# Strassen's algorithm in the down projection of an encoder layer's MLP, its products interleaved with the next group's up projection

## Chip, core and metric

The kernel runs on one core of a Trainium2 chip, with one launch. The metric is the device time of that launch in microseconds (us), the median of several runs. A difference of about 0.2% (5 us here) is what a measurement of this kernel can tell from no change. Five engines work side by side, each through its own list of instructions in order: TensorE (PE, matmul), VectorE (DVE), ScalarE (ACT), GpSimd (POOL) and SyncE (SP, which issues the transfers here).

## What is computed

One encoder layer on 512 tokens of width 2048, in float32: a token mixer (latent attention and a recurrent part), an output projection, and an MLP with 8192 hidden units. The change concerns the MLP.

```python
mix = jnp.concatenate([attn_out, rec_out], axis=-1) @ w_out[layer]
x = x + gate_a * _rmsnorm(mix, post_mix_g[layer])

h = _rmsnorm(x, pre_mlp_g[layer]) * (1.0 + scale_m) + shift_m
y = jnp.square(jax.nn.relu(h @ w_up[layer])) @ w_down[layer]
x = x + gate_m * _rmsnorm(y, post_mlp_g[layer])
```

`gate_m` is a part of `cond @ w_mod + b_mod`; the kernel keeps its product with `post_mlp_g` in a tile `G`, spread over all partitions.

## The kernel before

Float32 products are made from two reduced parts. Each operand is cast to a high part H by ACT (a CAST), and DVE subtracts H from the operand to give the low part L (`split` L205, `hl` L226). One product of a 128x128 stationary tile and a 128x512 moving tile is then three matmuls into the same accumulator (`mm3` L221: H·H, H·L, L·H). Weights come from memory in pieces of 512 KB into a ring of four tiles `raw`, and are split into rings of three `wH` and two `wL`, two DVE and two ACT instructions of 512 columns for each piece. `tc.high_priority` puts the loads and splits 35 places ahead in the scheduler's order.

**Ahead of the MLP**, `project_out` makes the output projection (tiles `wo`), and `residual(t)` takes token tile t (128 tokens) through the first residual sum (L973), the norm (ACT L976, DVE L978), 16 transposes on PE (`x2T`, L982, into a ring of three PSUM banks), the scaling to `hv` (DVE L991 and ACT L988) and the split of the result into `atH`/`atL` and `recH`/`recL`, which hold the MLP's input, feature-major.

**MLP** (L1005 to L1096). The hidden units are worked through in 16 groups of 512. `up(g)` makes 192 matmuls of 512 columns (16 k-tiles x 4 hidden tiles x 3) into four PSUM banks; `up(0)` is done in two token halves, 384 matmuls of 256 columns. ReLU by ACT, square by DVE and a split give `uH`, `uL`. `down(g)` makes 192 matmuls `dn` (4 column chunks x 4 token tiles x 4 k-tiles x 3), one PSUM bank for each token tile and chunk; DVE adds each bank into `y` (L1053, 16 of 512 columns a group; ACT copies in the first group, L1051). The order is up(g), then down(g-1). PSUM has a ring `mm` of five banks and a ring `sd` of three. The tile `G` is prepared in pieces (`units`, L1009), one after each up chunk of the groups from 2 on: sums over w_mod (`modacc`, L262), then a matmul with `ones` and two DVE operations with rows loaded from memory (L301 to L304).

**The end** is `down_last` for group 15: all eight pieces of w_down are loaded and split early, into `atH`/`recH`, which are free by then; then token tile by token tile 48 matmuls `dl`, the sum into `y` (L1080), the norm (L1082 to L1084) and the store (L1088).

Of the kernel before, what the change touches and what calls it, by code (L numbers as in the profile page):

```python
# [10 lines left out]
F32 = mybir.dt.float32  # L11
# [21 lines left out]
PRI = 35  # L33

# [12 lines left out]
def encoder_layer(ctx: ExitStack, tc: tile.TileContext, a, out):  # L47
# [13 lines left out]
    def psum(n_mm, n_sd):  # L61
        if banks:
            banks["ctx"].close()
        banks["ctx"] = ExitStack()
        banks["mm"] = banks["ctx"].enter_context(pool("mm", n_mm, space=PSUM))
        banks["sd"] = banks["ctx"].enter_context(pool("sd", n_sd, space=PSUM))
# [136 lines left out]
    def split(raw, n, parts=2):  # L203
        H = stream.tile([P, 1024], F32R, tag="wH", name="wH")
        L = stream.tile([P, 1024], F32R, tag="wL", name="wL", bufs=2)  # L205
# [34 lines left out]
    def mod_block(accs, spans, fin, own=None, pri=PRI):  # L240
# [11 lines left out]
        def step(c):  # L252
            def run():
                with tc.high_priority(offset=pri):
                    _, v = load(source(nk * c, nk), nk, w, own)
                    for k in range(nk):
                        kt = nk * c + k
                        if kt == 0:
                            st["acc"] = accs.tile([P, 1024], F32, tag="modacc", name="modacc", bufs=2)
# [33 lines left out]
    def to_row(dst, col, gv, gcol):  # L293
# [17 lines left out]
    with ExitStack() as ph:  # L311
# [251 lines left out]
        with pool("start", side="right") as stp:  # L563
# [8 lines left out]
            for i in range(len(bounds) - 1):  # L572
# [3 lines left out]
                mod.append(mod_block(hg, [(P * k0, w), (2048 + P * k0, w)],  # L576
# [77 lines left out]
        for i in range(4):  # L654
            units += mod_block(hg, [(3 * 2048 + 512 * i, 512), (4 * 2048 + 512 * i, 512)],
                               to_cols(blk(hb2, i), blk(hs2, i), blk(b_sm, i), blk(b_cm, i), blk(g_mlp, i), sdt))
# [282 lines left out]
    gp = ctx.enter_context(pool("gp"))  # L939
    G = gp.tile([P, D], F32, name="G")  # L940
    with ExitStack() as ph:
        wo = ph.enter_context(pool("wo"))
# [4 lines left out]
        for i in range(2):  # L947
            c = 2 * 2048 + 1024 * i
            units += mod_block(gp, [(c, 1024)], to_row(GA[:, 1024 * i:1024 * i + 1024], c, a["post_mix_g"], 1024 * i))
# [56 lines left out]
    with ExitStack() as ph:  # L1006
        ml = ph.enter_context(pool("ml"))
        y = ml.tile([P, NT, D], F32, name="y")
        units = []  # L1009
        for i in range(2):  # L1010
            c = 5 * 2048 + 1024 * i
            units += mod_block(gp, [(c, 1024)], to_row(G[:, 1024 * i:1024 * i + 1024], c, a["post_mlp_g"], 1024 * i))
        NG = FF // 512

        def up(g, halves=((0, 4),)):
            pss = [mmt(f"up{n}") for n in range(4)]
            for t0, t1 in halves:
                for k0 in range(0, KD, 2):
                    H, L = chunk([(wslice(w_up, k0, 2, 512 * g, 512), 512)], 2, 512)
                    interleave(units, 1 if g > 1 else 0)  # L1020
                    for n in range(4):
                        ns = slice(n * P, (n + 1) * P)
                        o = pss[n][:, t0 * P:t1 * P]
                        for k in range(2):
                            cH, cL, kk = cat(k0 + k)
                            mm3(o, H[:, k, ns], L[:, k, ns], cH[:, t0:t1, kk, :], cL[:, t0:t1, kk, :],
                                k0 + k == 0, k0 + k == KD - 1)
            uH = ml.tile([P, 4, S], F32R, tag="uH", name="uH", bufs=2)
            uL = ml.tile([P, 4, S], F32R, tag="uL", name="uL", bufs=2)
            for n in range(4):  # L1030
                r = ml.tile([P, S], F32, tag="relu", name="relu", bufs=2)
                nc.scalar.activation(r, pss[n], AF.Relu)
                nc.vector.tensor_tensor(r, r, r, ALU.mult)
                hl(uH[:, n, :], uL[:, n, :], r)
            return uH, uL

        def down(g, u):
            uH, uL = u
            for c in range(4):
                pss = [mmt(f"dn{t}") for t in range(NT)]  # L1040
                for k0 in range(0, 4, 2):
                    H, L = chunk([(wslice(w_down, 4 * g + k0, 2, 512 * c, 512), 512)], 2, 512)
                    for t in range(NT):
                        ts_ = slice(t * P, (t + 1) * P)
                        for k in range(2):
                            mm3(pss[t], uH[:, k0 + k, ts_], uL[:, k0 + k, ts_], H[:, k, :], L[:, k, :],
                                k0 + k == 0, k0 + k == 3)
                for t in range(NT):
                    yv = y[:, t, 512 * c:512 * c + 512]
                    if g == 0:  # L1050
                        nc.scalar.copy(yv, pss[t])  # L1051
                    else:
                        nc.vector.tensor_tensor(yv, yv, pss[t], ALU.add)  # L1053

        def down_last(g, u):
# [74 lines left out]
```

## Time and profile before

| quantity | before |
| --- | --- |
| median of 3 runs | 2499.7 us (2498.49 to 2500.56) |
| span of the profiled execution | 2501.2 us |
| PE busy | 2423.2 us (97%), 11702 matmuls and transposes |
| DVE busy | 1420.3 us (57%) |
| ACT busy | 835.8 us (33%) |
| moved by DMA | 341.81 MB, mean 137 GB/s |
| MLP | from 1073.88 us (first `up` matmul) to the end |

The profiled execution took 2501.2 us of span, 1.5 us above the median of the runs. Busy times of PE are sums of single instructions whose reported durations overlap (a 512-column matmul reports 0.39 us but the next begins 0.23 us later), so the page counts the union, and the pitch from start to start is what a matmul costs. Rows of the trace have the form: start, duration, engine, line, operation, out<-in, size, count, and in brackets the idle time just before with what ended it. A wait on an engine other than the one that sets the end costs nothing by itself.

### The profile page before, as it was taken

Reading aid. Unit: us, or ns where it says so; the run is one execution under the profiler, and the core shown is the slowest. Engines: PE = TensorE matmul, PEld = TensorE weight load, DVE = VectorE, ACT = ScalarE, POOL = GpSimd, SP = SyncE. Lnnn points to the kernel's source line nnn. Section 1 sums busy time; section 2 is a strip of 40 time slices with the busy share of each in tenths; the row PEclk is TensorE's granted clock in tenths of the full one; section 3 lists DMA queues with packets and bytes.
Section 4 is the critical chain, followed back from the end, with each engine's and each line's share of the span. In section 5 each row is a group of like instructions: output and inputs, shape, how many; then the busy total and the mean of one; then the engine's idle time right before and its main releaser. Section 6 shows DMA issues by size and latency. Waiting matters only on the chain.

```text
span 2501.2 us, 30421 instructions
## 1 busy us (share of the span) xinstructions
PE 2423.2 (97%) x11702; PEld 2011.8 (80%) x11702; DVE 1420.3 (57%) x2197; ACT 835.8 (33%) x1550; POOL 117.9 (5%) x127
## 2 busy tenths in 40 slices
PE   4999999999999999999999999999999999999998
PEld 3788898989877776788888888888888888888886
DVE  6974777677976765674454554434434433443456
ACT  5224333333454422563322222222222222222232
POOL 0110211111200000000000000000000000000000
PEclk9999999999999999999999999999999999999999
DMA  9863353445611177563544543333233333333334
GB/s 316 290 219 106 117 157 118 152 126 165 190 51 34 54 256 229 186 220 108 160 134 128 168 147 123 101 94 100 93 99 95 94 100 93 101 94 94 100 116 136
DMA packets 193228, 341.81 MB, mean 137 GB/s; under 512 B 16822, under 2 KB 65084, under 8 KB 191036
## 3 DMA queue, kind: packets, MB, share of 16 engines
q1 hardware_dynamic: 191888, 339.72, 43.3%
q8 instruction: 92, 1.51, 0.2%
q14 instruction: 52, 0.43, 0.1%
q10 hardware_dynamic: 1196, 0.16, 0.0%
HBM read 331.45 MB, written 8.39 MB: 136 GB/s over the span
## 4 chain that ended last, share of the span: by engine, by line
PE 65%; DMA 3%; DVE 2%; ACT 0%; issue 0%; DVEq 0%; ACTq 0%
PE up L224 9%; PE up L222 9%; PE up L223 9%; PE dn L222 9%; PE dn L224 9%; PE dn L223 9%; DMA raw<-in_w_mod_dram 2%; PE wo L223 1%; PE wo L224 1%; PE wo L222 1%; DVE modacc L262 1%; PE dl L222 1%; PE dl L224 1%; PE dl L223 1%; PE pT L888 1%; PE sc L870 1%
## 5 line engine op out<-in xcount | busy, mean ns | idle before, releaser
L209 DVE TENSOR_TENSOR wL<-raw,wH 128x512 fp32r<-128x512 f32 (+1 forms) x800 | 529.4, 700 | 664.6 <-issue 533.4
L208 ACT CAST wH<-raw 128x512 fp32r<-128x512 f32 (+1 forms) x800 | 457.7, 616 | 1258.9 <-PE up L223 463.2
L222 PE MATMUL dn<-wH,uH 128*128 128x512 f32 x960 | 374.2, 390 | 0.0
L223 PE MATMUL dn<-wL,uH 128*128 128x512 f32 x960 | 374.2, 390 | 0.0
L224 PE MATMUL dn<-wH,uL 128*128 128x512 f32 x960 | 373.6, 389 | 0.0
L262 DVE SCALAR_TENSOR_TENSOR modacc<-raw,cond,modacc 128x1024 f32<-128x1024 f32 x120 | 160.5, 1338 | 109.0 <-DMA raw<-in_w_mod_dram 108.4
L224 PEld LDWEIGHTS dn<-wH,uL 128*128 128x128 f32 x960 | 180.2, 188 | 38.3 <-issue 0.5
L223 PEld LDWEIGHTS dn<-wL,uH 128*128 128x128 f32 x960 | 180.2, 188 | 38.3 <-issue 0.7
L222 PEld LDWEIGHTS dn<-wH,uH 128*128 128x128 f32 x960 | 180.2, 188 | 37.7 <-issue 0.2
L224 PE MATMUL up<-recH,wL 128*128 128x512 f32 (+1 forms) x544 | 207.8, 382 | 0.0
L222 PE MATMUL up<-recH,wH 128*128 128x512 f32 (+1 forms) x544 | 207.6, 382 | 0.0
L223 PE MATMUL up<-recL,wH 128*128 128x512 f32 (+1 forms) x544 | 207.5, 381 | 0.0
L224 PE MATMUL up<-atH,wL 128*128 128x512 f32 (+1 forms) x544 | 203.9, 377 | 2.8 <-DVE wL L209 2.8
L222 PE MATMUL up<-atH,wH 128*128 128x512 f32 (+1 forms) x544 | 205.1, 378 | 0.0
L223 PE MATMUL up<-atL,wH 128*128 128x512 f32 (+1 forms) x544 | 204.7, 377 | 0.0
L1053 DVE TENSOR_TENSOR y<-y,dn 128x512 f32<-128x512 f32 x224 | 152.8, 685 | 80.2 <-PE dn L224 80.2
L224 PEld LDWEIGHTS up<-recH,wL 128*128 128x128 f32 x544 | 102.0, 188 | 22.1
L222 PEld LDWEIGHTS up<-recH,wH 128*128 128x128 f32 x544 | 102.0, 188 | 21.9
L223 PEld LDWEIGHTS up<-recL,wH 128*128 128x128 f32 x544 | 102.0, 188 | 21.9
L224 PEld LDWEIGHTS up<-atH,wL 128*128 128x128 f32 x544 | 102.0, 189 | 21.7 <-DVE wL L209 3.0
L222 PEld LDWEIGHTS up<-atH,wH 128*128 128x128 f32 x544 | 102.6, 189 | 18.9 <-issue 0.2
L223 PEld LDWEIGHTS up<-atL,wH 128*128 128x128 f32 x544 | 102.5, 188 | 18.9 <-issue 0.2
(352 smaller groups left out, 3943.9 us busy)
## 6 DMA issues: line engine op xcount, KB each, us to landing
raw<-in_w_up_dram SPq DMA_DIRECT2D x136, 512.0 KB, 3.7
raw<-in_w_mod_dram SPq DMA_DIRECT2D x128, 512.0 KB, 4.1
raw<-in_w_down_dram SPq DMA_DIRECT2D x128, 512.0 KB, 3.7
raw<-in_w_in_dram SPq DMA_DIRECT2D x128, 256.0 KB, 3.1
mraw<-in_w_mod_dram SPq DMA_DIRECT2D x48, 512.0 KB, 5.4
raw<-in_w_out_dram SPq DMA_DIRECT2D x40, 512.0 KB, 4.1
raw<-in_w_in_dram SPq DMA_DIRECT2D x24, 512.0 KB, 6.4
mraw<-in_w_mod_dram SPq DMA_DIRECT2D x32, 256.0 KB, 4.1
```

Source lines behind the costliest of these rows:

```text
L208: nc.scalar.copy(H[:, o], raw[:, o])
L209: nc.vector.tensor_tensor(L[:, o], raw[:, o], H[:, o].bitcast(F32), ALU.subtract)
L222: nc.tensor.matmul(o, s_h, m_h, start=first, stop=False)
L223: nc.tensor.matmul(o, s_h, m_l, start=False, stop=False)
L224: nc.tensor.matmul(o, s_l, m_h, start=False, stop=last)
L262: nc.vector.scalar_tensor_tensor(st["acc"][:, :w], v[:, k, :], cond[:, kt:kt + 1], st["acc"][:, :w], ALU.mult, ALU.add)
L870: nc.tensor.matmul(ps, QS[t][0:64, hd, :], KX[0:64, :], start=False, stop=True)
L888: nc.tensor.transpose(pt[:, k * P:(k + 1) * P], pe[:, k * P:(k + 1) * P], ident)
L1053: nc.vector.tensor_tensor(yv, yv, pss[t], ALU.add)
```

## The change

The down projection of groups 0 to 14 is made by Strassen's algorithm in Winograd's form. For each group and each of two column chunks the 4 k-tiles x 512 tokens of `u` are cut into blocks A (2 k-tiles x 256 tokens) and the w_down pieces into blocks B (256 x 512); seven products of blocks take the place of eight. Each product is 12 matmuls of 512 columns into a PSUM tile of two banks, `dn`; three of the seven go on in the accumulator of an earlier one. So a group's down projection has 14 products, 168 matmuls. Sums of blocks are made on DVE: four of A a group (128x512 each, in place in `u`) and eight of B (128x1024, in place in the loaded tiles). A second accumulator `V` takes the part that belongs to three quarters of the output and is added to `y` once, in `down_last`, by three operations of 128x2x1024.

Which instructions follow which is written by hand: three strings give for each group 22 steps, U for one piece of the next group's up projection (24 matmuls), D for one product. Weights are split two steps ahead (`LEAD`), loads of w_down run up to six products ahead into a ring `B` of five tiles. A piece is now split by one ACT and one DVE instruction of 1024 columns; H has a ring of four places and L one of three. PSUM is set up anew ahead of the MLP: four banks `up` and two sets `dn` of two banks. The pieces for `G` go through tiles of the ring `B` and through the sets `dn`. `up(0)` stays 384 matmuls of 256 columns, group 15 stays as it was (192 matmuls, now in the four `up` banks). The tiles of `to_row` move to a pool that is closed before the MLP, and a scratch area is made smaller, which moves addresses alone.

```diff
+FIRST = "UUUUDDUDDUDDUDDUDDDDDD"
+ROUND = "UDUDDUDUDDUDUDDUDUDDDD"
+LAST = "UUDUUDUDUDUDUDDDDDDDDD"
...
+    psum(8, 0)
...
+        V = ml.tile([P, 2, 1024], F32, name="V")
...
+        def btile(name):
+            return ml.tile([P, 1024], F32, tag="B", name=name, bufs=NB)
+
+        def ubank(n):
+            return banks["mm"].tile([P, 512], F32, tag="up", name=f"up{n}", bufs=4)
+
+        def dset(name):
+            return banks["mm"].tile([P, 1024], F32, tag="dn", name=name, bufs=2)
...
+                    bg = btile("modbg")
+                    nc.sync.dma_start(bg[:, 0:512],
+                                      a["b_mod"][0:1, col + o:col + o + 512].partition_broadcast(P)[:, 0, :])
...
+                    ps = dset("modr")
+                    nc.tensor.matmul(ps[:, 0:512], ones, acc[:, o:o + 512], start=True, stop=True)
...
+            split_form("A11", A11)
+            split_form("A22", A22)
+            nc.vector.tensor_tensor(A22, A21, A22, ALU.add)
+            split_form("S1", A22)
+            split_form("A12", A12)
+            nc.vector.tensor_tensor(A21, A11, A21, ALU.subtract)
+            nc.vector.tensor_tensor(A11, A22, A11, ALU.subtract)
+            nc.vector.tensor_tensor(A12, A12, A11, ALU.subtract)
+            split_form("S4", A12)
+            split_form("S3", A21)
+            split_form("S2", A11)
...
+            goes_on = {2: 0, 3: 1, 6: 4}.get(f)
+            X = sets[f] = sets.pop(goes_on) if goes_on is not None else dset(f"dn{f}")
+            for t in range(2):
+                o = X[:, 512 * t:512 * t + 512]
+                ts_ = slice(t * P, (t + 1) * P)
+                for k in range(2):
...
+                    nc.tensor.matmul(o, sh, mh, start=first, stop=False, skip_group_check=skip)
+                    nc.tensor.matmul(o, sh, ml_, start=False, stop=False, skip_group_check=skip)
+                    nc.tensor.matmul(o, sl, mh, start=False, stop=last, skip_group_check=skip)
...
+            if g == 0 and fresh:
+                nc.scalar.copy(dst, Xv)
+            else:
+                nc.vector.tensor_tensor(dst, dst, Xv, ALU.add)
...
+            nc.vector.tensor_tensor(y[:, 0:2, 1024:], y[:, 0:2, 1024:], V, ALU.add)
+            nc.vector.tensor_tensor(y[:, 2:4, :1024], y[:, 2:4, :1024], V, ALU.add)
+            nc.vector.tensor_tensor(y[:, 2:4, 1024:], y[:, 2:4, 1024:], V, ALU.add)
...
+            fm = make_forms(hidden(pss))
+            pss = [ubank(i) for i in range(4)]
+            for _ in range(22):
+                ahead(n + 1 + LEAD)
+                what, _, i = steps[n]
+                H, L = wts.pop(n)
+                if what == "U":
+                    up_mms(pss, i, H, L, 0, NT)
+                    if g > 0:
+                        interleave(units, 1)
+                else:
+                    product(i, fm, H, L)
+                n += 1
+        down_last(NG - 1, pss)
```

Up to the end of the output projection the instructions stand in the same order on every engine. Three places show what moves behind it.

On PE at the start of the MLP (`wo` output projection, `up` the first up projection, `x2T` transposes of token tiles 2 and 3), before, in the middle of the first half of up(0), whose first matmul directly follows the last `wo`:

```order
L222 MATMUL up_8957<-atH,wH 128x256
L223 MATMUL up_8957<-atL,wH 128x256
L224 MATMUL up_8957<-atH,wL 128x256
L982 MATMUL x2T<-ident,xr 128x128 x12
L222 MATMUL up_8954<-atH,wH 128x256
L223 MATMUL up_8954<-atL,wH 128x256
L224 MATMUL up_8954<-atH,wL 128x256
```

and now:

```order
L230 MATMUL wo_8659<-wH,atH 128x512
L231 MATMUL wo_8659<-wL,atH 128x512
L232 MATMUL wo_8659<-wH,atL 128x512
L992 MATMUL x2T<-ident,xr 128x128 x32
L230 MATMUL up_8961<-atH,wH 128x256
L231 MATMUL up_8961<-atL,wH 128x256
```

The 32 transposes, which stood in five lots among the matmuls of up(0), now all stand ahead of its first one.

On DVE in the middle of the MLP, where down(g-1) runs, before (`dn` banks added to `y`, `wL` splits of weights, `modacc` a sum for G):

```order
L1053 TENSOR_TENSOR y<-y,dn_11573 128x512
L209 TENSOR_TENSOR wL<-raw,wH 128x512 x2
L1053 TENSOR_TENSOR y<-y,dn_11574 128x512
L209 TENSOR_TENSOR wL<-raw,wH 128x512 x2
L1053 TENSOR_TENSOR y<-y,dn_11643 128x512
L1053 TENSOR_TENSOR y<-y,dn_11644 128x512
L1053 TENSOR_TENSOR y<-y,dn_11645 128x512
L209 TENSOR_TENSOR wL<-raw,wH 128x512 x2
L1053 TENSOR_TENSOR y<-y,dn_11646 128x512
```

and now, around the four products that close a group (L1093 squares, `fL` splits of blocks of A, `dn_13843` the fourth product's set, `dn_13962` the fifth and seventh product's, `dn_13982` the sixth's):

```order
L1191 TENSOR_TENSOR y<-y,dn_13823 128x2x512
L1093 TENSOR_TENSOR u<-u 128x1024
L236 TENSOR_TENSOR fL<-u,fH 128x512
L236 TENSOR_TENSOR wL<-B_13552,wH 128x1024
L1093 TENSOR_TENSOR u<-u 128x1024
L236 TENSOR_TENSOR wL<-B_13651,wH 128x1024
L1191 TENSOR_TENSOR y<-y,dn_13843 128x2x512
L236 TENSOR_TENSOR fL<-u,fH 128x512
L1191 TENSOR_TENSOR y<-y,dn_13962 128x2x512
L236 TENSOR_TENSOR wL<-raw,wH 128x1024
L236 TENSOR_TENSOR wL<-B_13837,wH 128x1024
L1191 TENSOR_TENSOR V<-V,dn_13982 128x2x512
```

The additions of PSUM into `y` are now of two banks and stand among squares and splits of the next group, where before they stood between splits alone.

On DVE at the end, before (`atL`, `recL` the held splits of w_down, `dl` the last group's banks):

```order
L228 TENSOR_TENSOR atL<-raw,atH 128x1024
L228 TENSOR_TENSOR recL<-raw,recH 128x1024 x3
L1053 TENSOR_TENSOR y<-y,dn_18100 128x512
L228 TENSOR_TENSOR recL<-raw,recH 128x1024
L1053 TENSOR_TENSOR y<-y,dn_18101 128x512
L1053 TENSOR_TENSOR y<-y,dn_18102 128x512
L1053 TENSOR_TENSOR y<-y,dn_18103 128x512
L1080 TENSOR_TENSOR y<-y,dl_18207 128x512
```

and now (`upl` the last group's banks, L1210 to L1212 the additions of `V`):

```order
L236 TENSOR_TENSOR fL<-u,fH 128x512 x2
L236 TENSOR_TENSOR atL<-lraw,atH 128x1024
L1191 TENSOR_TENSOR y<-y,dn_17825 128x2x512
L236 TENSOR_TENSOR atL<-lraw,atH 128x1024 x3
L236 TENSOR_TENSOR recL<-lraw,recH 128x1024 x3
L1210 TENSOR_TENSOR y<-y,V 128x2x1024
L236 TENSOR_TENSOR recL<-lraw,recH 128x1024
L1211 TENSOR_TENSOR y<-y,V 128x2x1024
L1212 TENSOR_TENSOR y<-y,V 128x2x1024
L1226 TENSOR_TENSOR y<-y,upl_17929 128x512
```

Seven of the eight held splits now stand behind the last product's addition, and the three additions of `V` ahead of the first addition of `upl`.

## Rows read from the trace of the kernel before

**Rows 1.** The page: busy time, share, instructions; granted TensorE clock in 40 slices.

```profile
PE 2423.2 (97%) x11702; PEld 2011.8 (80%) x11702; DVE 1420.3 (57%) x2197; ACT 835.8 (33%) x1550; POOL 117.9 (5%) x127
PEclk9999999999999999999999999999999999999999
```

**Rows 2.** Busy per stretch: PE, PEld, DVE, ACT, POOL, clock, DMA share, GB/s.

```profile
1136.60:2446.80 1310.20, 1310.20 (x5730) 1074.69 (x5729) 581.67 (x863) 354.45 (x616) 0.00 (x0) 1.00 0.36 111
2000.00:2087.00 87.00, 87.00 (x382) 71.45 (x381) 36.03 (x56) 22.79 (x40) 0.00 (x0) 1.00 0.32 97
```

**Rows 3.** Waits from 1130 to 2400: total us, times, longest us.

```profile
ACT wH L208 <- PE up L223: 447.6, 104, 5.0
```

**Rows 4.** Timeline of PE (start, duration, what): down matmuls, then the last twelve.

```profile
1999.81 0.39 PE L222 MATMUL dn<-wH,uH 128*128 128x512 f32 x1
...
2006.38 0.39 PE L224 MATMUL dn<-wH,uL 128*128 128x512 f32 x1
...
2488.73 0.39 PE L222 MATMUL dl<-recH,uH 128*128 128x512 f32 x1
...
2491.29 0.40 PE L224 MATMUL dl<-recH,uL 128*128 128x512 f32 x1
```

**Rows 5.** Timeline of PE at the start of the MLP.

```profile
1073.88 0.28 PE L222 MATMUL up<-atH,wH 128*128 128x256 f32 x1
...
1083.57 0.38 PE L224 MATMUL up<-atH,wL 128*128 128x256 f32 x1 [2.82 <-DVE wL L209]
...
1121.77 0.28 PE L224 MATMUL up<-recH,wL 128*128 128x256 f32 x1
...
1127.89 0.40 PE L222 MATMUL up<-atH,wH 128*128 128x512 f32 x1
```

**Rows 6.** Timeline of DVE: scaling and split of tokens 0, 1; residuals of 2, 3.

```profile
1057.61 0.73 DVE L991 TENSOR_SCALAR hv<-x2T,hs,hb 128x128 f32<-128x128 f32 x2
...
1060.83 1.29 DVE L228 TENSOR_TENSOR recL<-hv,recH 128x512 fp32r<-128x512 f32 x2
1062.04 0.73 DVE L991 TENSOR_SCALAR hv<-x2T,hs,hb 128x128 f32<-128x128 f32 x2
...
1078.05 4.86 DVE L973 SCALAR_TENSOR_TENSOR mix<-mix,r,xr 128x1024 f32<-128x1024 f32 x4
...
1086.03 1.28 DVE L978 TENSOR_SCALAR xr<-mix,r 128x2048 f32<-128x2048 f32 x1
```

**Rows 7.** Timeline of PE after a wait, the first and the last slow matmul.

```profile
1067.45 0.65 PE L982 MATMUL x2T<-ident,xr 128*128 128x128 f32 x4 [2.48 <-ACT hv L988]
1067.86 0.67 PE L223 MATMUL wo<-wL,atH 128*128 128x512 f32 x1
...
1071.31 0.44 PE L223 MATMUL wo<-wL,atH 128*128 128x512 f32 x1
```

**Rows 8.** Two stretches with or behind a wait of PE, columns as in rows 2.

```profile
1050.00:1055.00 5.00, 3.99 (x24) 3.46 (x25) 5.00 (x12) 4.42 (x8) 0.00 (x0) 1.00 0.90 304
...
1085.00:1090.00 5.00, 5.00 (x32) 5.00 (x31) 4.68 (x10) 3.04 (x7) 0.00 (x0) 0.66 0.68 216
```

**Rows 9.** Groups by line and shape, 1136 to 2380: busy us, mean ns, idle before.

```profile
L1053 DVE TENSOR_TENSOR y<-y,dn 128x512 f32<-128x512 f32 x208 | 142.1, 685 | 77.0 <-PE dn L224 77.0
...
L1032 ACT ACTIVATE relu<-up 128x512 f32<-128x512 f32 x56 | 33.4, 596 | 11.4 <-PE up L224 11.4
...
L303 DVE TENSOR_TENSOR G<-modr,modb 128x512 f32<-128x512 f32 x4 | 2.8, 690 | 3.5 <-DMA modb<-in_b_mod_dram 3.1 <-PE modr L301 0.4
```

**Rows 10.** The same from 2380 to the end, DVE, 1024 columns.

```profile
L228 DVE TENSOR_TENSOR recL<-raw,recH 128x1024 fp32r<-128x1024 f32 x4 | 4.9, 1226 | 2.3 <-ACT recH L227 2.2
```

**Rows 11.** The same, ACT.

```profile
L227 ACT CAST recH<-raw 128x1024 fp32r<-128x1024 f32 x4 | 4.2, 1049 | 4.3 <-DMA raw<-in_w_down_dram 4.3
```

**Rows 12.** Timeline of DVE at 2443: a split of 1024 and its follower.

```profile
2443.57 1.23 DVE L228 TENSOR_TENSOR recL<-raw,recH 128x1024 fp32r<-128x1024 f32 x1 [1.03 <-ACT recH L227]
2444.71 0.68 DVE L1053 TENSOR_TENSOR y<-y,dn 128x512 f32<-128x512 f32 x1
```

More of the change, by code (lines that the diff above doesn't have):

```diff
@@ L291, in to_cols, with to_row @@
         return fin
[L293 removed]
+    def to_row(gp, dst, col, gv, gcol):
         def fin(acc):
@@ L1037, in down @@
[L1037 to L1053, printed above, removed]
@@ new lines, in encoder_layer, with form_tiles, hidden @@
+        FORMS = ["A11", "S1", "A12", "S4", "S3", "S2", "A22"]
+        def form_tiles(f):
+            return [ml.tile([P, 2, HALF], F32R, tag=f"f{x}{f}", name=f"f{x}", bufs=1) for x in "HL"]
+        def hidden(pss):
+            u = ml.tile([P, 4, S], F32, tag="u", name="u", bufs=1)
+            for n in range(4):
+                nc.scalar.activation(u[:, n, :], pss[n], AF.Relu)
+            for n in (0, 2):
+                nc.vector.tensor_tensor(u[:, n:n + 2, :], u[:, n:n + 2, :], u[:, n:n + 2, :], ALU.mult)
+            return u
@@ new lines, in encoder_layer, with down_loads, product @@
+        loaded = [0]
+        def down_loads(q):
+            while loaded[0] < min(q, NP):
+                s, f = divmod(loaded[0], 7)
+                for b in LOADS.get(f, []):
+                    down_load(s, b)
+                loaded[0] += 1
+        sets = {}
+        def product(q, fm, H, L):
+            s, f = divmod(q, 7)
+            g, c = divmod(s, 2)
+            fH, fL = fm[FORMS[f]]
+            goes_on = {2: 0, 3: 1, 6: 4}.get(f)
[3 more added lines that the diff above has]
+                ts_ = slice(t * P, (t + 1) * P)
+                for k in range(2):
+                    first, last = k == 0 and goes_on is None, k == 1
+                    sh, sl, mh, ml_ = fH[:, k, ts_], fL[:, k, ts_], H[:, k, :], L[:, k, :]
+                    skip = goes_on is not None
+                    nc.tensor.matmul(o, sh, mh, start=first, stop=False, skip_group_check=skip)
+                    nc.tensor.matmul(o, sh, ml_, start=False, stop=False, skip_group_check=skip)
+                    nc.tensor.matmul(o, sl, mh, start=False, stop=last, skip_group_check=skip)
+            cs = slice(512 * c, 512 * c + 512)
+            c2 = slice(1024 + 512 * c, 1024 + 512 * c + 512)
+            dst, fresh = [(V[:, :, cs], True), (y[:, 2:4, c2], True), (y[:, 0:2, cs], True), (y[:, 0:2, c2], True),
+                          (y[:, 2:4, c2], False), (V[:, :, cs], False), (y[:, 2:4, cs], True)][f]
+            Xv = X.rearrange("p (t n) -> p t n", t=2)
+            if g == 0 and fresh:
+                nc.scalar.copy(dst, Xv)
+            else:
+                nc.vector.tensor_tensor(dst, dst, Xv, ALU.add)
@@ L1057, in down_last @@
+        def down_last(g, pss):
+            u = hidden(pss)
+            uu = []
+            for n in range(4):
+                fH, fL = [t.rearrange("p k s -> p (k s)") for t in form_tiles(FORMS[n])]
+                hl(fH, fL, u[:, n, :])
+                uu.append((fH, fL))
             held = []
```

177 lines of the change are left out of this document (125 added, 52 removed).

## Prediction

> **What bounds the kernel now.** I read the page first, then the stretch of the MLP, then the waits, then single rows. The page shows PE busy for 97% of the span at full clock in nearly every slice, DVE for 57% and ACT for 33% [rows 1]. In the MLP it is stricter: from 1136.6 to 2446.8 PE is busy in all of the 1310.2 us, at a granted clock of 1.00, the upper level of 2.4 GHz, while DVE is busy 581.7 us and ACT 354.5 us [rows 2]. The waits say the same from the other side: ACT, the engine that casts the weights, waited 447.6 us for PE to free a buffer, and no wait of PE of any size is listed [rows 3]. So between 1136 and 2447 time is the number of matmuls times their pitch, and the other engines have slack. One matmul of the down projection costs (2006.38 - 1999.81) / 29 = 0.2266 us, not its reported 0.39; with `recH` as stationary tile it is (2491.29 - 2488.73) / 11 = 0.2327 [rows 4]. Outside that stretch, at the start of the MLP and at its end, PE depends on chains through DVE and ACT, and the change moves work there too.
>
> **What is removed.** 15 groups x (192 - 168) = 360 `dn` matmuls of 512 columns, all on the path that sets the end: 360 x 0.2266 = **-81.6 us**. The up projection, the last group and what lies ahead of the MLP keep their counts. The new stationary tiles are splits of blocks of `u` as before; I take the same pitch. Were it 0.2327, the 15 x 168 = 2520 remaining products would cost 2520 x 0.0061 = 15.4 us more.
>
> **Start of the MLP: +16 us.** Before, `up(0)` started at 1073.88, at once behind the output projection, and ended at 1127.89, with one wait of 2.82 us inside [rows 5]; it worked on tokens 0 and 1 while tokens 2 and 3 went through the residual on DVE and ACT. Now PE has the 32 transposes of tokens 2 and 3 ahead of the first up matmul, and these need the norms. The chain in the old trace: the four residual sums run 1078.05 to 1082.91, and the scaling of token 3 begins at 1086.03 [rows 6]. Without the weight splits that stood between, I put its end at 1086.7. Then come eight units of scaling and split, in pairs, through a ring of three PSUM banks, so the last transposes wait for the third pair's scaling. A pair took 1062.04 - 1057.61 = 4.43 us [rows 6] with weight splits between; these are gone from the list. Of DVE's own work a pair holds two lots of 0.73 and one of 1.29, 2.7 us, and between the ends of 2.7 and 4.4 I take 3.95, near the upper one, as each step there waits for ACT and back. So the third pair begins at 1086.8 + 7.9 = 1094.7, its scaling ends at 1096.6, and the first up matmul stands at about 1097. 384 matmuls of 256 columns cost (1127.89 - 1121.77) / 52 = 0.1177 each [rows 5], since 52 matmuls lie between, so 45.2 us. A wait of some 20 us is followed by a spell at the lower clock: behind a wait of 2.48 us eight steps took 1071.31 - 1067.86 = 3.45 us instead of 1.81 [rows 7], so 1.7 us more. End: 1097 + 45.2 + 1.7 = 1143.9 against 1127.89, **+16**. Ends: 12, with pairs at 2.7 us, and 22, with a pair at 4.43 and one or two waits such as the 2.82 us for the splits, which now stand on DVE behind the whole chain.
>
> **The groups: +1 us.** By 1024 columns a DVE operation reports 1.226 us [rows 10] but its follower starts 2444.71 - 2443.57 = 1.14 us after it [rows 12]; two of 512 take 1.29 in a row, so 0.6 each [rows 6]. DVE's list in a group: 22 splits, 8 sums of B, 14 additions, 2 squares, 46 x 1.14 = 52.4, and 11 operations of 512, 6.7; 59 us. PE: 96 up matmuls at 0.2266, 96 at 0.2327 and 168 products, 82.2 us. ACT has fewer instructions than before for the same columns (1.05 us for 1024 [rows 11]). DVE fits with 23 us to spare, so it is order that can hurt. The addition of two banks is not in the trace: one bank costs 0.685 [rows 9], so two lie between 1.14 (SBUF, 1024 columns) and 1.37 (twice); I take 1.14, the row of the same size. A product lasts 12 x 0.2266 = 2.72 us, and one that opens a set waits until the set before it in the ring of two is added. I walked one group through; only one place is tight, its four closing products. Counted from the start of the last up piece: its banks close at 1.4, 2.8, 4.2 and 5.5; the second ReLU (0.596 [rows 9]) ends at 3.7; then DVE has in order square (4.9), form split (6.2, behind ACT's cast), weight split (7.35), square (8.5), weight split (9.6), and the fourth product's addition to 10.8. The sixth product wants that set at 5.54 + 2 x 2.74 = 11.0. So 0.2 us of margin: no wait at my prices. At the full 1.226 for each of the five operations of 1024 each group waits 0.25 us, with 1.37 for the addition besides 0.5: 4 to 8 us in all. Taken: 1, ends 0 and 8. Cover: the weight splits are two steps ahead of PE; transfers are the same 16 pieces of 512 KB a group.
>
> **The pieces for G: +3 us.** The sums come over the same ring B as w_down and the row through a set `dn`; the next product but one waits until DVE has added the bias rows, which come by DMA into a tile that must first be free. Before, DVE idled 3.1 us for these rows [rows 9], hidden as PE had other banks. Now that idle time reaches PE: 3, ends 0 and 8 (two blocks, each once the 3.1 and a product's length, with overlap).
>
> **The end: +10 us.** From the last up piece PE has nine products, 24.5 us, and 48 matmuls of token tile 0, 11.0; then, at 35.5, the fifth tile wants a bank that the first addition of `upl` must free. DVE has in that time 2 squares, 7 splits, 4 sums, 9 additions and 8 held splits, 30 x 1.14 = 34.2, four splits of 512, 2.4, and three additions of V at twice 1.14, 6.8: 43.4. With 0.3 to start and 0.6 for the addition that frees the bank: 44.3, so PE stands for 8.8 us; a slow spell behind it adds 1.7 [rows 7]. Taken 10; ends 6 (the first square and two splits run before the piece ends) and 14 (1.226 for each). Before, the held splits had run early and PE did not wait. The norm and the stores behind the last matmul are the same.
>
> **Sum.** -81.6 + 16 + 1 + 3 + 10 = -51.6. On the profiled span 2501.2 that is 2449.6; the runs' median is 1.5 below that span, so I give 2499.7 - 51.6 = **2448 us**. With the ends of the four terms (18 to 52 against 30) the forecast's own range is 2436 to 2470.
>
> **Rivals.**
> 1. *Cheap ends.* The chain of tokens 2 and 3 overlaps better than in any row, and DVE works off more of the last list before the last up piece ends: terms 10, 0, 0 and 4, so 2432. For it: DVE's own work in a pair is 2.7 us only. Against: the pairs alternate between DVE and ACT.
> 2. *A slow spell in every group.* If the tight place does make PE wait and the clock falls to its lower level (1.2 GHz) each time, 1.7 us x 14 and the waits of 0.25, 3.5: +26, so about 2473. Against it: in 1050 to 1055 PE idled 1.0 us and the clock stayed at 1.00; it fell to 0.66 in 1085 to 1090 behind 2.82 us [rows 5, 8]. My walk gives no wait over 0.5.
> The Trainium skill, "TensorE: Matmul & The Clock Gate", section "A second HAM failure mode: psum-queue depth-cycling", speaks against this change: cycling through PSUM banks leaves PE idle for short moments between groups of matmuls, often enough that the clock swings. The rows at 1050 do not bear it out for one wait of that size; nothing here shows repeated ones.
> 3. *The gain does not arrive whole, by pitch.* Products at 0.2327: 2448 + 15 = 2463. Against: the rise is seen with `recH` alone.
> 4. *Slower than before: PE waits for its two sets.* In each group six products open a set close behind another. If the two-bank addition or its queue is late at three of them by enough to bring a slow spell, that is 3 x 1.7 x 15 = 77 us and more: about 2525. It decides from two such spells a group (2 x 1.7 x 15 = 51, the whole net gain), or from an addition of 3.0 us, at which DVE's 59 + 14 x 1.9 passes PE's 82 by 3.4 a group. For it: only two sets. Against: the rows put the addition at 1.14 to 1.37, at which the tightest place waits 0.5 us at most and the others not at all.
>
> **Chances.** Forecast with its own range 0.64; rival 1 below it 0.10; rival 2 0.12; rival 3 0.05, inside or just by the range; rival 4 0.06; within 0.2% (2494.7 to 2504.7, about what a measurement can tell from no change) 0.03, a mixture of 2 and 4. So faster 0.91, same 0.03, slower 0.06. The range 2434 to 2475 takes in rivals 2 and 3 and leaves about 0.2 out.
>
> **What will show it.** In the profile after: `dn` matmuls 2520, pitch 0.2266; the first `up` at about 1097 and the first 512-column `up` at 1144; PE busy without gaps in a group of 82.2 us, clock 1.00; DVE's two-bank addition at 1.2 to 1.4 us; a PE wait of about 9 us for DVE at the fifth `upl` tile. The prediction is wrong if PE shows a wait in every group, if the clock in the groups falls under 1.00, or if the first `up` starts soon after 1074.

## The result

| | before | changed |
| --- | --- | --- |
| median of 4 runs | 2499.1 us (2495.2 to 2500.6) | 2454.9 us (2451.4 to 2456.2) |
| ratio | | 0.982, 95% interval 0.9806 to 0.9835 |
| span of the profiled execution | 2501.2 us | 2449.6 us |
| PE busy | 2423.2 us (97%) | 2348.0 us (96%) |
| DVE busy | 1420.3 us (57%) | 1783.2 us (73%) |

The kernel is 44 us (1.8%) faster by the medians. The forecast was 2448 us, range 2434 to 2475, from a span of 2449.6; the span came out at 2449.6. That the two agree to a tenth is chance, as the ledger below shows: several terms missed by 1 to 4 us and cancelled. The profiled execution of the changed kernel is also the fastest of its four runs (the other three lie 3 to 5 us above it), while that of the kernel before, with a span of 2501.2, is longer than any of the four runs beside it. So the two traces lie 51.6 us apart and the medians 44.2; the 7 us between are scatter of single executions, and the ledger can't tell in which of its rows they lie.

The page of the changed kernel, beside [rows 1]:

```profile
PE 2348.0 (96%) x11342; PEld 1944.7 (79%) x11342; DVE 1783.2 (73%) x2203; ACT 932.9 (38%) x1423; POOL 119.2 (5%) x127
...
PEclk9999999999999999989999999999999999999998
```

PE has 360 instructions fewer, DVE as many as before but 363 us more to do, since more of them have 1024 columns. The clock has a lower slice at the start of the MLP and one at its end.

All waits of PE behind the output projection (total us, times, longest us):

```profile
PE x2T L992 <- DVE xr L988: 10.4, 1, 10.4
PE x2T L992 <- ACT hv L998: 6.3, 3, 2.9
PE upl L230 <- DVE y L1226: 3.6, 1, 3.6
PE upl L231 <- DVE recL L236: 2.2, 2, 1.7
PE dn L1180 <- DVE G L1047: 1.8, 3, 0.9
PE upl L231 <- DVE atL L236: 1.1, 2, 0.7
PE dn L1180 <- ACT wH L235: 0.7, 1, 0.7
PE dn L1181 <- DVE wL L236: 0.5, 1, 0.5
```

Three places are named, and they are the three of the forecast: the transposes ahead of the first up projection, the pieces for G, and the last group. No other wait is listed in the groups.

Where the 51.6 us between the two spans lie, by the starts of the same matmuls in both traces (the ledger's rows stand here and in the next sections; those of before are [rows 4, 5] and the first `dn` behind the last up piece of before, at 2403.69):

| stretch on PE | before | after | matmuls saved | beyond that |
| --- | --- | --- | --- | --- |
| up to the end of the output projection | 1073.9 | 1070.2 | | -3.7 |
| up(0) | 54.0 | 71.0 | | +17.0 |
| first 512-column up to the end of the last up piece | 1275.8 | 1218.4 | 276, -62.5 | +5.1 |
| from there to the end of the last matmul | 87.8 | 80.5 | 84, -19.0 | +11.7 |
| norm and stores behind it | 9.7 | 9.5 | | -0.2 |

```profile
2403.69 0.40 PE L222 MATMUL dn<-wH,uH 128*128 128x512 f32 x1
```

```profile
1069.97 0.39 PE L232 MATMUL wo<-wH,atL 128*128 128x512 f32 x1
...
1080.74 2.79 PE L992 MATMUL x2T<-ident,xr 128*128 128x128 f32 x12 [10.38 <-DVE xr L988]
...
1093.64 0.56 PE L230 MATMUL up<-atH,wH 128*128 128x256 f32 x1
...
1141.21 0.40 PE L230 MATMUL up<-atH,wH 128*128 128x512 f32 x1
...
2359.35 0.40 PE L232 MATMUL up<-recH,wL 128*128 128x512 f32 x1
...
2405.14 0.79 PE L230 MATMUL upl<-atH,fH 128*128 128x512 f32 x1 [3.56 <-DVE y L1226]
...
2439.82 0.40 PE L232 MATMUL upl<-recH,fL 128*128 128x512 f32 x1
```

The first `dn` behind the last up piece of before, and then the timeline of PE after the change: the output projection's last matmul, the wait, the first up matmul at 1093.64, the first of 512 columns at 1141.21, the last up matmul, the wait for the first addition of the last group, and the last matmul.

The groups by stretch (PE, PEld, DVE, ACT, POOL busy; clock, DMA share, GB/s), then the end:

```profile
2359.59:2440.05 80.46, 72.40 (x301) 56.69 (x299) 70.20 (x84) 28.01 (x52) 0.00 (x0) 0.96 0.43 137
1141.21:2359.59 1218.38, 1216.60 (x5303) 994.06 (x5302) 912.10 (x864) 440.29 (x498) 0.00 (x0) 1.00 0.37 116
```

In the groups PE is busy all but 1.8 of 1218.4 us at a clock of 1.00, as in [rows 2]; DVE, then at 44%, is now at 75%. At the end DVE is busy 70.2 of 80.5 us and PE stands for 8.

### The profile page after: what moved, and what is told of

It reads as the page before. It is cut to its first block, busy times and chain, and to the rows that moved or that the text cites. A ratio compares the mean times of both kernels' runs of the same rounds, so it can differ in the third digit from the quotient of the medians.

```text
span 2449.6 us, 29645 instructions
## 1 busy us (share of the span) xinstructions
PE 2348.0 (96%) x11342; PEld 1944.7 (79%) x11342; DVE 1783.2 (73%) x2203; ACT 932.9 (38%) x1423; POOL 119.2 (5%) x127
## 4 chain that ended last, share of the span: by engine, by line
PE 62%; DMA 3%; DVE 3%; ACT 1%; issue 1%; DVEq 0%; ACTq 0%
PE up L232 10%; PE up L230 10%; PE up L231 10%; PE dn L1180 8%; PE dn L1182 8%; PE dn L1181 7%; DMA raw<-in_w_mod_dram 2%; PE wo L231 1%; PE wo L232 1%; PE wo L230 1%; DVE modacc L273 1%; PE pT L899 1%; PE sc L881 1%; PE upl L230 0%; PE upl L231 0%
## 5 line engine op out<-in xcount | busy, mean ns | idle before, releaser
L235 ACT CAST wH<-B 128x1024 fp32r<-128x1024 f32 x210 | 221.1, 1054 | 499.3 <-PE up L231 194.3
L236 DVE TENSOR_TENSOR wL<-B,wH 128x1024 fp32r<-128x1024 f32 x210 | 256.5, 1222 | 185.4 <-issue 69.8
L1180 PE MATMUL dn<-wH,fH 128*128 128x512 f32 x840 | 329.3, 392 | 2.5 <-DVE G L1047 1.8
L1182 PE MATMUL dn<-wH,fL 128*128 128x512 f32 x840 | 327.5, 390 | 0.0
L1181 PE MATMUL dn<-wL,fH 128*128 128x512 f32 x840 | 326.8, 389 | 0.5 <-DVE wL L236 0.5
L216 ACT CAST wH<-raw 128x512 fp32r<-128x512 f32 (+1 forms) x288 | 163.2, 611 | 340.9 <-PE wo L232 59.5
L217 DVE TENSOR_TENSOR wL<-raw,wH 128x512 fp32r<-128x512 f32 (+1 forms) x288 | 199.1, 725 | 88.0 <-issue 44.6
L236 DVE TENSOR_TENSOR wL<-raw,wH 128x1024 fp32r<-128x1024 f32 x136 | 165.9, 1221 | 95.0 <-issue 43.0
L1181 PEld LDWEIGHTS dn<-wL,fH 128*128 128x128 f32 x840 | 157.7, 188 | 34.7 <-DVE wL L236 1.0
L1191 DVE TENSOR_TENSOR y<-y,dn 128x1024 f32<-128x1024 f32 x142 | 172.2, 1212 | 0.1
```

The lines of the kernel that those rows point to most:

```text
L216: nc.scalar.copy(H[:, o], raw[:, o])
L217: nc.vector.tensor_tensor(L[:, o], raw[:, o], H[:, o].bitcast(F32), ALU.subtract)
L235: nc.scalar.copy(h_out, src)
L236: nc.vector.tensor_tensor(l_out, src, h_out.bitcast(F32), ALU.subtract)
L1180: nc.tensor.matmul(o, sh, mh, start=first, stop=False, skip_group_check=skip)
L1181: nc.tensor.matmul(o, sh, ml_, start=False, stop=False, skip_group_check=skip)
```

## The experiments

### The start of the MLP: what holds back the first up projection

The forecast put the +16 us down to the new order on PE, in which all transposes stand ahead of the first up matmul. This run takes that away: the first up projection uses banks of the old PSUM rings.

```diff
-    psum(8, 0)
...
-        pss = [ubank(n) for n in range(4)]
+        pss = [mmt(f"up{n}") for n in range(4)]
...
+        u = hidden(pss)
+        psum(8, 0)
```

> The first up projection writes into banks of the old PSUM rings, and PSUM is set up anew only behind its ReLU; nothing else is altered. Theory (the new set-up of PSUM ahead of the first up projection is what puts the 32 transposes of tokens 2 and 3 ahead of it, and that order costs the time): the first up matmul follows the last matmul of the output projection at once, up(0) takes 54 us instead of 71.0, and the kernel is 15 to 18 us faster than the changed one: span 2432 to 2435, ratio to the kernel before about 0.975. Rival (the residual chain of tokens 2 and 3 sets the time whatever the order, and the second half of up(0) waits for it): up(0) stays over 65 us, less than 6 us are gained.

Measured: 2451.3 us, ratio 0.9816 (0.9801 to 0.983), against 0.982 for the change itself: nothing gained that the runs can tell. These are the numbers that the rival named, but not its cause, as the run with both locks off shows below. The order did change, and the time went elsewhere:

```profile
1068.90 0.28 PE L230 MATMUL up<-atH,wH 128*128 128x256 f32 x1
...
1082.98 2.82 PE L992 MATMUL x2T<-ident,xr 128*128 128x128 f32 x12 [7.21 <-DVE xr L988]
...
1100.56 0.58 PE L232 MATMUL up<-atH,wL 128*128 128x256 f32 x1 [6.27 <-DVE wL L236]
...
1141.13 0.50 PE L230 MATMUL up<-atH,wH 128*128 128x512 f32 x1
```

The first up matmul now follows the output projection at once, at 1068.90, but the third piece stands at 1100.56 for a low part from DVE, and up(0) ends at 1141.13, 72.2 us after it began. DVE's list of that stretch shows why:

```profile
1097.60 0.69 DVE L236 TENSOR_TENSOR recL<-hv,recH 128x512 fp32r<-128x512 f32 x1
1098.68 0.69 DVE L236 TENSOR_TENSOR recL<-hv,recH 128x512 fp32r<-128x512 f32 x1 [0.39 <-ACT recH L235]
1099.29 3.49 DVE L236 TENSOR_TENSOR wL<-raw,wH 128x1024 fp32r<-128x1024 f32 x3
```

The third and all later splits of w_up stand behind the last split of tokens 2 and 3. In the code, the change gives the splits an extra H and an extra L tile (`xH`, `xL`) in the MLP's own pool; the third L is the first to go there. By the code that pool is opened when the residual's is closed, so its tiles can lie where the residual's were and then wait for them; no row shows the addresses, and it is the next two runs that show the effect. So there is a second lock. One run takes off only this one, another both (and has the additions of V moved, next section).

```diff
+            if not own:
+                H = stream.tile([P, 1024], F32R, tag="wH", name="wH", bufs=3)
+                L = stream.tile([P, 1024], F32R, tag="wL", name="wL", bufs=NWL)
+                hl(H, L, src)
+                return [t.rearrange("p (k n) -> p k n", k=2) for t in (H, L)]
...
-            return split_next(raw)
+            return split_next(raw, g > 0)
```

> The splits of the first up projection use only the rings that exist before the MLP (three H, two L), not the extra H and L tile that lie in the memory which the residuals of tokens 2 and 3 still hold; PSUM is set up anew where the change has it. Theory (two locks, each enough by itself to hold the first up projection back: the order of the transposes through PSUM, and these tiles; the run with the PSUM edit alone gained under 2 us): this edit alone gains under 3 us as well, the first up matmul stays behind the transposes at 1090 or later. Rival (the tiles are the only true cause, the transposes' order follows them): up(0) ends some 15 us earlier than in the changed kernel.

Measured, one run: 2456.3 us, and the first up matmul at 1091.31 behind all transposes, up(0) 71.1 us long. The rival, that the tiles alone are the cause, falls.

> PSUM set up behind the first up projection, its splits in the old rings alone, and the additions of V moved as in the run on them. Theory (two locks): up(0) starts with the end of the output projection and takes 52 to 58 us instead of 71 to 72.8, as before the change; against the run with the additions of V moved 13 to 18 us less: span 2426 to 2431, ratio to the kernel before 0.971 to 0.974. Rival (with both locks off DVE, which now splits by 1024 columns among the residual's steps, sets the time): 62 us and more, span over 2436.

Measured: 2436.1 us, ratio 0.9758 (0.9742 to 0.9775), 8.8 us under the run with V alone, which is less than expected; but the first up projection did what the theory says:

```profile
1069.86 0.28 PE L230 MATMUL up<-atH,wH 128*128 128x256 f32 x1
...
1123.91 0.50 PE L230 MATMUL up<-atH,wH 128*128 128x512 f32 x1 [2.16 <-ACT u L1095]
...
1574.55 0.79 PE L1184 MATMUL dn<-wH,fH 128*128 128x512 f32 x1 [6.16 <-DVE G L1046]
1575.14 0.63 PE L1185 MATMUL dn<-wL,fH 128*128 128x512 f32 x1
```

up(0) takes 1123.91 - 1069.86 = 54.05 us, as before the change [rows 5]: 17 us back. The residual chain of tokens 2 and 3 is the same as in the change, so it is not what sets the time by itself. Of the 17 us, 7.4 were lost again in the groups (1225.4 us against 1218.0 in the run with V alone): the wait of 6.16 and a spell at the lower clock (pitch 0.43 from 1575.14 on). The run with only the ring edit shows that longer wait for G as well (6.32 us). So each lock by itself holds the start back by the full 17 us, and only both together free it.

### The end: the list of DVE behind the last up piece

```diff
-            nc.vector.tensor_tensor(y[:, 0:2, 1024:], y[:, 0:2, 1024:], V, ALU.add)
-            nc.vector.tensor_tensor(y[:, 2:4, :1024], y[:, 2:4, :1024], V, ALU.add)
-            nc.vector.tensor_tensor(y[:, 2:4, 1024:], y[:, 2:4, 1024:], V, ALU.add)
...
+                    if (t, c) in ((0, 2), (1, 3), (2, 1)):
+                        v = {0: y[:, 0:2, 1024:], 1: y[:, 2:4, :1024], 2: y[:, 2:4, 1024:]}[t]
+                        nc.vector.tensor_tensor(v, v, V, ALU.add)
```

> The three additions of V stand behind the first additions of the last group's banks of the token tile that needs them, instead of ahead of all. Theory (DVE's list between the last up piece and the fifth bank is what PE waits for): 6.6 us leave that list, the wait of 3.56 us at the fifth bank and the slow spell behind it go, the shorter waits for the held splits stay: 4 to 6 us faster than the changed kernel, span 2444 to 2446. Rival (the held splits, with the loads behind them, are what comes last): the wait stays where it is by over half, under 2 us gained. Second rival: the additions only move the wait to the later token tiles: the fifth bank is free, but waits of 2 us stand at token tiles 1 to 3, nothing gained.

Measured: 2444.9 us, ratio 0.9789 (0.9775 to 0.9804), 6.4 us under the run with the PSUM edit of the same chip and 10 under the changed kernel's own median. The waits of its last group:

```profile
PE upl L231 <- DVE atL L236: 1.1, 2, 0.7
PE upl L231 <- DVE recL L236: 0.9, 2, 0.8
PE upl L230 <- ACT recH L235: 0.8, 1, 0.8
PE dn L1181 <- DVE wL L236: 0.5, 1, 0.5
PE dn L1180 <- ACT wH L235: 0.4, 1, 0.4
```

The wait of 3.56 us at the fifth bank is gone; 3.7 us for splits stay. Nothing turned up at the later token tiles. The spell at a pitch of 0.43 did not go with the wait, as the theory had it. It stands at the same place, behind two short waits, in the profiled execution of this run:

```profile
2396.88 0.50 PE L230 MATMUL upl<-recH,fH 128*128 128x512 f32 x1 [0.81 <-ACT recH L235]
2398.14 0.50 PE L231 MATMUL upl<-recL,fH 128*128 128x512 f32 x1 [0.76 <-DVE recL L236]
...
2399.57 0.63 PE L230 MATMUL upl<-atH,fH 128*128 128x512 f32 x1
```

The spell lasts until 2402.56. So of the 5.8 us between the spans (2449.6 and 2443.8) 4.4 lie behind the last up piece, which is what the waits shrank by. With both this and the PSUM edit alone:

> Both edits together. Theory: they touch different ends of the MLP, so the gains add: 20 to 24 us faster than the changed kernel, span 2426 to 2430, ratio to the kernel before about 0.972. Rival: part of one is given back in the other (for instance in transfers): under 17 us.

Measured: 2446.8 us, ratio 0.9796 (0.9779 to 0.9812), no better than V alone. That was to be expected once the PSUM edit by itself gave nothing; it is the same miss a second time. Here the last group has no such spell.

### The pieces for G

```diff
+        def begin():
+            st["acc"] = accs("modacc")
+            nc.sync.dma_start(st["acc"], bias)
+            nc.vector.tensor_scalar(st["acc"], st["acc"], 1.0 / P, None, ALU.mult)
...
-                    nc.vector.tensor_tensor(d, ps[:, 0:512], bg[:, 0:512], ALU.add)
-                    nc.vector.tensor_tensor(d, d, bg[:, 512:1024], ALU.mult)
+                    nc.vector.tensor_tensor(d, ps[:, 0:512], d, ALU.mult)
...
+        nc.sync.dma_start(G, a["post_mlp_g"][0:1, :].partition_broadcast(P)[:, 0, :])
```

> On top of the run with both locks off: the row b_mod for G is loaded into the tile of the sums before they begin (scaled by 1/128, so that the sum over partitions gives it once), and the gain row straight into G; so no load stands between the matmul with ones and the product that wants its set. Theory (PE's waits of 0.31, 0.48 and 6.16 us behind the additions for G, and the slow spell behind the longest, come from these loads): these waits go, 6 to 9 us less than with both locks off: span 2424 to 2427, ratio to the kernel before about 0.973. Rival (the wait is for the sums themselves or for the ring B, and moves to another step): under 3 us.

Measured: 2424.2 us, ratio 0.9704 (0.9685 to 0.9723), 11.9 us under the run with both locks off. In the groups no wait of PE is left:

```profile
1123.00:2350.00 1227.00, 1227.00 (x5347) 1003.63 (x5346) 921.36 (x870) 442.75 (x500) 0.00 (x0) 1.00 0.37 114
```

The waits were 6.95 us, the restarts and the spell some 2.6 us more. In the two traces 8.4 us of the difference lie in the groups, and 3.8 ahead of the MLP, where the output projection ended earlier (1066.0 against 1069.9); the edit touches nothing there, so that part is put down to scatter. This version is 30.7 us faster than the change and 72 us (3.0%) faster than the kernel before.

> As the run before it, with the last string UUDUUDUUDUUDDDDDDDDDDD instead of UUDUUDUDUDUDUDDDDDDDDD: the last up piece stands one product further ahead. Theory (DVE's list behind the last up piece is what PE waits for in the last group, 3.0 us in six waits): PE has 2.72 us more to do meanwhile, the waits shrink to about 1 us: 2 us less. Rival (each wait is for one split that follows one load, however far the up piece is ahead): no difference over 1 us.

Measured: 2424.0 us, ratio 0.9706 (0.9692 to 0.9721). No difference that the runs can tell. The two waits for pieces of the products shrank from 1.2 to 0.5 us, but those for the held splits did not, and all waits of the last group together are 3.2 us as before; for the held splits the rival holds.

### What the arithmetic is worth, and what the order

The changed kernel's frame with eight ordinary products instead of seven (four splits of weights for eight products, no sums of blocks, no V):

```diff
-        FORMS = ["A11", "S1", "A12", "S4", "S3", "S2", "A22"]
+        FORMS = ["A11", "A21", "A12", "A22"]
...
-ROUND = "UDUDDUDUDDUDUDDUDUDDDD"
+ROUND = "UDDUDDUDDUDDUDDUDDUDDUDD"
```

> The changed kernel's frame (steps U and D by hand, two-bank sets, 1024-column splits, loads ahead, the old PSUM edit) with the ordinary eight products in two sets a group and column chunk, 16 products and 192 matmuls a group as before; no block sums, no V, 8 additions a group instead of 14. Theory (the gain is the 360 matmuls, the frame by itself costs): 81.6 us come back, 6.8 us of V and 2 us of pitch go from the end and the groups: 2449.6 + 81.6 - 6 = 2525, slower than the kernel before by about 1% (24 us). Rival (the interleaved order is itself a gain): no slower than the kernel before.

Measured: 2519.9 us, ratio 1.0091 (1.0071 to 1.0111). The theory holds: the frame by itself is 22 us slower than the kernel before. The two traces are 17.1 us apart, and most of that is the start of the MLP: up(0) ends 14.1 us later, the stretch from the first 512-column up to the last matmul (1142.00 to 2508.45) is 1366.5 us against 1363.4 before, with one wait of 0.6 us. The changed kernel needs 1298.6 there, 67.8 less. So of the 81.6 us of saved matmuls, 67.8 arrive and 13.8 are lost. By the ledger these are the last group, the waits for G and the pitch; with eight products PE has no wait in the last group at all.

The same products as in the change, but with all up pieces of a group ahead of its products:

```diff
-ROUND = "UDUDDUDUDDUDUDDUDUDDDD"
+ROUND = "UUUUUUUUDDDDDDDDDDDDDD"
```

> Strassen's products, but all eight up pieces of a group ahead of its 14 products (all three strings 8 U, then 14 D). Theory (DVE needs about 50 of its 59 us a group in the 38 us in which PE makes the products, the splits run only two steps ahead): PE waits 8 to 14 us in each of 15 groups and the clock drops behind some of these waits: span 2580 to 2680, granted clock in the groups under 0.97. Rival (the slack of 23 us a group is enough wherever the products stand): under 2 us of wait a group, span under 2480.

Measured, one run: 2452.7 us, as fast as the change (2451.4 to 2456.2), and not one wait of PE in the groups. The rival holds, and my count was wrong: I had put 50 us of DVE work into the 39 us of the products. The stretch of one group's products (columns as above):

```profile
1932.10:1971.10 39.00, 39.00 (x173) 32.03 (x172) 37.89 (x34) 16.09 (x17) 0.00 (x0) 1.00 0.34 105
```

DVE is busy 37.9 of 39.0 us: nearly all splits and sums of the blocks of A and three of the eight sums of blocks of B are made while PE is at the up pieces, so the products just cover the rest. The interleaving is not what the change gains by; but without it DVE has 1.1 us of slack in 39.

### A dearer addition

```diff
+                for _ in range(1):
+                    nc.vector.tensor_scalar(Xv, Xv, 1.0, None, ALU.mult)
                 nc.vector.tensor_tensor(dst, dst, Xv, ALU.add)
```

> Each addition of a product's two banks is preceded by a DVE operation on the same two banks that multiplies them by 1.0 in place (not in the first group where ACT copies), so the price of freeing a set is about doubled, 1.14 to about 2.3 us. Theory (order walk: 0.2 us of margin at one place of a group, the sixth product, and 23 us of slack in all): DVE takes about 75 us of 82 in a group, PE waits about 1 us at the sixth product of a group and nowhere else by much, 14 to 20 us in all, and the clock in the groups stays at 1.00: span 2464 to 2475. Rival (two sets are too few, so that a dearer addition stops PE at several products of a group): 3 waits a group of 1 us and more, span over 2500. Rival (short waits in every group bring the clock to its lower level): granted clock in the groups under 0.95.

Measured, one run: 2481.4 us, span 2479.6, 30 us over the change. The added operation took 1.227 us. Its waits in the groups:

```profile
PE dn L1180 <- DVE G L1047: 5.5, 2, 3.2
PE dn L1180 <- DVE V L1193: 4.0, 1, 4.0
PE up L232 <- DVE wL L236: 1.8, 2, 1.1
PE up L230 <- ACT wH L235: 1.6, 2, 1.1
PE modr L1045 <- DVE modacc L273: 0.3, 1, 0.3
```

They all lie in the groups with G, between 1397 and 1604; the other groups have none, at DVE busy in 277 of 300 us (1900 to 2200). Of the 30 us, 18 lie ahead of the end of the last up piece, and 12 behind it, where PE waits 15.8 us instead of 8.1. Neither theory nor rivals are borne out: the wait expected at the sixth product of each group isn't there. The run is no clean test of it, since the scheduler, which saw the longer chain, put the closing products among up matmuls (from 1986.35 on a product, 3 up matmuls, a product, 10 up matmuls, a product). What it does show is that DVE can be at 92% without PE waiting.

## Why the prediction was right, point by point

The forecast of the median, 2448, is 7 us under the measured one, though the span was met. The step from span to median is where that lies: it took the median 1.5 us below the profiled span, as in the kernel before, but the changed kernel's profiled execution was its fastest, with a median 5.3 us above its span.

- **Matmuls.** 360 fewer at 0.2266: as forecast. The prediction calls `recH` the stationary tile of the slower matmuls; it is the moving one (`mm3` takes the stationary tile ahead of the moving one and is given the weights there in the up projection; the rows name the moving tile first). In the products of the change the moving tiles are splits of weights as in the old `dn`, so the conclusion stands. The pitch of `dn` was 0.2277 on the mean instead of 0.2269, 2 us over 2520 matmuls, an eighth of what the third rival held possible for each.
- **Start, +16.** Measured 71.0 - 54.0 = +17.0. A pair of scalings takes 1090.92 - 1086.93 = 3.99 us, where 3.95 was taken from between 2.7 and 4.4; in each pair DVE stands 1.3 us for ACT (0.27 and 1.03), as was argued. The first up matmul came at 1093.64 instead of 1097, since the output projection ended 3.7 us earlier; behind it, 23.4 us against 23.1. The 384 matmuls took 47.6 us, 2.4 over their full pitch instead of the 1.7 for a spell at the lower clock (PE, PEld, DVE, ACT, POOL busy; clock, DMA share, GB/s):

```profile
1070.20:1093.60 23.40, 6.75 (x33) 5.58 (x33) 18.55 (x34) 15.66 (x33) 0.00 (x0) 0.65 0.56 197
1093.60:1104.00 10.40, 10.40 (x73) 10.40 (x72) 7.49 (x11) 6.19 (x11) 0.00 (x0) 0.80 0.21 56
1104.00:1141.20 37.20, 37.20 (x315) 37.20 (x315) 16.50 (x14) 15.27 (x16) 0.00 (x0) 1.00 0.81 255
```

The granted clock is 0.80 in the first 10 us of up matmuls. The size was right; the cause was half of it. The step "Now PE has the 32 transposes of tokens 2 and 3 ahead of the first up matmul" named one of two locks; the splits that stand on DVE behind the whole chain were in the text, but as a wait of 2.8 us at the upper end, not as a lock worth the whole term.
- **Groups, +1.** No wait was measured in the ordinary groups, at a margin close to the 0.2 us of the walk. In the group at 1961 the fourth product's addition and the sixth product's first matmul are:

```profile
1965.06 1.21 DVE L1191 TENSOR_TENSOR y<-y,dn 128x1024 f32<-128x1024 f32 x1
```

```profile
1966.58 0.40 PE L1180 MATMUL dn<-wH,fH 128*128 128x512 f32 x1
```

The addition ends at 1966.27, 0.3 us ahead. Its price is 1.21 us reported, and the next operation on DVE starts 1.13 later, the lower end of the bracket of 1.14 to 1.37. So what the tight place needed was the case, and rivals 2 and 4 had no ground: two sets are enough at this price. (Rival 2's own sum, 23.8 + 3.5 in place of 1, gives 2474, not 2473.) That the margin holds at a dearer addition too was not shown.
- **G, +3.** Waits of 1.8 us in all, some 2.4 with the restarts; with the 2 us of pitch that is 4.4 of the 5.1 us that the ledger has for the groups. The mechanism was right (the run with the loads ahead takes the waits away), and its upper end of 8 is near what two of the variants show, where PE stood for over 6 us and DVE's addition waited for the load to the last (3.30 us in the run with both locks off).
- **End, +10.** Measured +11.7 by the ledger. Instead of one wait of 8.8 us at the fifth bank there were seven of 8.1 in all, of which 3.56 there. The price of DVE's list was right: the fifth bank was free 45.5 us after the last up piece, where 44.3 was forecast. What the prediction left out is that PE would be held up on its way there by the held splits, which it put into the list but not into PE's path: PE came to the fifth bank after 42.0 us instead of 35.5, with six waits of 4.5 us behind it. Several of these do not come from the length of DVE's list. The casts by ACT that the held splits need stood for their loads, and DVE for the casts:

```profile
2394.44 1.05 ACT L235 CAST recH<-lraw 128x1024 fp32r<-128x1024 f32 x1 [2.41 <-DMA lraw<-in_w_down_dram]
```

```profile
2395.52 1.23 DVE L236 TENSOR_TENSOR recL<-lraw,recH 128x1024 fp32r<-128x1024 f32 x1 [1.56 <-ACT recH L235]
```

The run with the additions of `V` moved takes 4.4 us of waits away; 3.7 us stay, and moving the last up piece did not shrink the part for the held splits. What holds these loads back was not tried. The spell behind the longest wait cost 1.7 (eight matmuls from 2405.14 to 2408.65), as the row of the old trace gave.
- **Not forecast: -3.7 us.** The old trace has a wait of 2.48 us at the end of the output projection and a spell behind it [rows 7]; in the new one the same transposes have no wait (1065.81). In the traces of the changed kernel and its ten variants that wait is 0 in nine, 0.21 in one and 1.23 in another, and the output projection ends anywhere from 1066.0 to 1071.2. So it varies by 5 us from trace to trace, and one old trace can't show how much of the 3.7 us belongs to the change.
- **Rival 2 and the Trainium skill.** With 14 products a group cycling through two sets the clock was 1.00 over 1218 us, and PE stood for 1.8 us in all of them. The rule of the Trainium skill in "TensorE: Matmul & The Clock Gate", section "A second HAM failure mode: psum-queue depth-cycling", which spoke for a swinging clock, tells of a bf16 kernel and starts from short idle moments of PE between groups of matmuls. PE had none between products here, so the rule itself was not put to the test; what is shown is that cycling through two sets need not leave PE idle. Nor do these runs show that the length of one wait decides whether the clock falls. In the change, waits of 0.2 to 1.7 us were followed by matmuls at full pitch and that of 3.56 us by 3 us at a pitch of 0.43; in the run with both locks off 6.16 us were followed by 5 us at that pitch, but 2.16 us by none; in the run with V alone the spell came behind waits of 0.81 and 0.76 us.

## What to carry to other kernels

Count what an algorithmic saving brings by the pitch of the saved work, and then walk the places where the steady order begins and ends: here the steady part gave all but 5 of its 62.5 us, and both the larger losses and the later 30 us of gain lay in the first 70 us, the last 80 us and one side job of a few DVE operations. A tile that is added to a ring from a new pool may lie in memory that an earlier stage still holds; as the code reads, that is why the third split of w_up stood behind the whole residual here, and keeping the first splits to the old ring was one half of the cure. And a delay may be held by two causes, each enough alone; taking one away and seeing no gain doesn't acquit it.

## What had not been expected of the hardware

The pitch of a down matmul depends on what ran ahead of it: behind an up piece with `recH` as moving tile the first six or so `dn` matmuls still take about 0.232 us, then 0.2267 (in the timeline from 2359.59 on, and in products behind such pieces in each group: mean 0.230 for the product against 0.2267 for others). So the slower pitch, which the prediction had tied to `recH` alone, isn't a matter of that tile alone. The cause stays open. It makes the mean 0.2277 here, since products now follow such pieces several times a group, where before they did once.
